# Block sums of three weight matrices: DRAM transfers, or adds in SBUF beside the split

## The chip, the cores and the metric

One core of a Trainium2 chip runs the whole program in one launch. The metric is the device time of one execution in microseconds (us), lower is better. A change of under 0.3% (7.1 us) counts here as no change.

## What is computed

A decoder layer on 1024 tokens of width 1024, in float32. Cut to its matrix products (`u` is the normalised and modulated input):

```python
mod = silu(c) @ w_ada + b_ada                       # 6 rows: shift, scale, gate, twice
hq, hf, hi, hg, rq, rk, rv, rg, ga, gb = split(u @ w_in)
ya = hgrn2(hq, hf, hi, hg) @ w_pa                   # 8 recurrent heads, chunks of 64
yb = retention(rq, rk, rv, rg) @ w_pb               # 4 heads, chunks of 128, gated by silu(rg)
x  = layer_norm(a * x + (1 + gate1) * ((sigmoid(ga) * ya + sigmoid(gb) * yb) @ w_o))
u  = x * (1 + scale2) + shift2
x  = layer_norm(a * x + (1 + gate2) * (square(relu(u @ w_up + b_up)) @ w_down + b_down))
```

## The kernel before

Every float32 operand is split into a high and a low half (`split`, L180-182: ACT copies the high half, DVE subtracts it to get the low one), and every product is three matmuls, high by high, high by low, low by high (`mm3`, L184-194, whose matmuls stand in the profile at L186, L187 and L188).

**Stages, by time in the profiled execution.** To 67 us the start; to about 650 us the HGRN2 heads, with the projection of `ga` at their end; to 1175 us the four retention heads (`r_head`); to 1427 us the gates (`gates`: `gb` in two parts of 256 columns, `rg` in four); then the merge with `w_pa` and `w_pb`, `w_o` (from 1635 us), the up projection (1748 to 2060 us, eight parts) and the down projection.

**Seven products.** Gates, merge, up and down projection use a scheme of seven block products instead of eight. It needs, of a weight with blocks w11, w12, w21, w22, four sums beside three plain blocks: `q5` = w21+w22, `q6` = w11+w21+w22, `q7` = w11+w21, `q3` = w12 + `q6`'s sum; `q1`, `q2`, `q4` are w11, w12, w22. The activations have the like sums, made by DVE (`t_sums`, L932 to L948) as the stage begins. A part of the gates or of the up projection is worked on in the order q1 q5 q6 q2 q7 q3 q4; the first two parts together begin q1 q1 q2 q2, then q5 q6 q7 q3 q4 of the one and of the other (the lead parts below). Each product is 24 matmuls of 128x512.

**Who makes the sums of the weights.** `block_sums` (L197-218) writes, for all six weights (28 parts), four copies and four accumulating transfers of 512 KB from DRAM to DRAM, issued on POOL's queue (L207, L208): 224 transfers. `mm3` paces them: after every `PREP` = 14 x 512 columns of matmuls the next transfer is issued, and it waits for the matmul of that moment (`after`, L226). They begin at 70.5 us and the last is issued at 1166 us, in the order `gb`, `rg`, `pa`, `pb`, `up`, `dn`. In the dense stretches one goes out about every 3.4 us. DMA work of the stages that POOL issues (takes and puts of head outputs, small rows) stands in the same queue.

**The weight stream.** Weights come in pieces of 512 KB through SP's queue into tiles `raw` with three buffers (`_load`, L271-276), always up to three pieces ahead; `_split_to` (L278) splits each piece into `wh` and `wl`, three buffers each, two tiles ahead of the product that asks for one (`W`, L301). In the retention stage the stream also holds the pieces of `w_ada` for the second half of the layer: DVE multiplies them straight out of `raw` (`ada_step`, L378; `ada_group`, L897), eight steps to a group, in order with the rest of its work. The names in the profile's rows: `in_w_ada`, `in_w_in`, `in_w_up` are weights in DRAM, `up_s`, `dn_s`, `gb_s`, `rg_s` their sums, `psa` to `psd` PSUM banks, `ru` the activation sums, `q5h`/`q5l` and so on their halves, `o` a product's copy in SBUF, `hv` the head outputs that the gates take back from DRAM.

Of the kernel before, what the change touches and what calls it, by code (L numbers as in the profile page):

```python
# [9 lines left out]
F32 = mybir.dt.float32  # L10
# [4 lines left out]
ALU = mybir.AluOpType  # L15
# [3 lines left out]
P = 128  # L19
# [12 lines left out]
C_RQ, C_RK, C_RV, C_RG = 4096, 5120, 6144, 8192  # L32
C_GA, C_GB = 10240, 11264
# [28 lines left out]
DN_ORDER = ("q1", "q5", "q6", "q3", "q7", "q2", "q4")  # L62
SECOND = ("q2", "q5", "q3")


def group_steps(parts):

# [5 lines left out]
GATE_STEPS = group_steps([("gb", p) for p in range(2)] + [("rg", p) for p in range(4)])  # L73
UP_STEPS = group_steps([("up", p) for p in range(8)])
LAST = 4
PREP = 14 * 512

H_DEFER = (3, 8)
H_ORDER = (("hq", "hf", "hg", "hi"), ("hg", "hi", "hq", "hf"))
# [68 lines left out]
class Trunk:  # L148
# [45 lines left out]
        return r, l  # L194


    def block_sums(self, name, w, cut, n):  # L197


        nc = self.nc  # L200
        kh, nh = w.shape[0] // 2, w.shape[1] // 2
        st = (nh if cut else kh) // n
        part = (lambda a, p: a[:, st * p:st * (p + 1)]) if cut else (lambda a, p: a[st * p:st * (p + 1), :])
        w11, w12, w21, w22 = ([part(w[k * kh:(k + 1) * kh, m * nh:(m + 1) * nh], p) for p in range(n)]
                              for m in (0, 1) for k in (0, 1))
        s1, s2, s3, s4 = ([self.dp.tile(list(w11[0].shape), F32, name=f"{name}_s{j}_{p}") for p in range(n)] for j in range(1, 5))
        copy = lambda d, a: self.sums.append((0, lambda: nc.gpsimd.dma_start(d, a)))  # L207
        add = lambda late, d, a: self.sums.append((late, lambda: nc.gpsimd.dma_start(d, a, accum_op=ALU.add, max_dma_last_dim=8192)))  # L208
        for p in range(n):
            copy(s1[p], w21[p])  # L210
            copy(s2[p], w11[p])
            copy(s3[p], w11[p])
            copy(s4[p], w12[p])
            add(1, s1[p], w22[p])
            add(1, s3[p], w21[p])
# [28 lines left out]
    def spec_N(self, w, r0, c0, key):  # L244
# [2 lines left out]
        tiles = [(key + (i,), [((lambda d: d.rearrange("p (k c) -> p k c", k=4)), i, (lambda a: a))]) for i in (0, 1)]  # L247
        return pcs, tiles

    def spec_1(self, ap, key):  # L250
        return [ap], [(key, [((lambda d, a=ap: d if len(a.shape) == 2 else d.rearrange("p (k c) -> p k c", k=a.shape[1])), 0, (lambda a: a))])]

    def build_stream(self, specs):
        self.w_tiles = []
        self.w_pcs = []
        for pcs, tiles in specs:
            base = len(self.w_pcs)
            self.w_pcs += pcs
            for key, ops in tiles:
                self.w_tiles.append((key, [(d, base + i, s) for d, i, s in ops]))  # L260
        self.w_raw = {}
        self.w_dst = {}
        self.w_done = {}
        self.w_next = self.w_split = self.w_load = 0
# [13 lines left out]
    def _split_to(self, n):  # L278
        while self.w_split < min(n, len(self.w_tiles)):
            key, ops = self.w_tiles[self.w_split]  # L280
            self._load_to(max(i for _, i, _ in ops) + 3)
            if key[0] == "ada":
                self.w_done[self.w_split] = [self.w_raw[i] for _, i, _ in ops]
                self.w_split += 1
                continue
            if key[0] == "wo":
                self.split(self.woh[key[1]], self.wol[key[1]], self.w_raw[ops[0][1]])
                self.w_done[self.w_split] = None
                self.w_split += 1
# [1148 lines left out]
def build(ctx, tc, ins, out):  # L1438
    k = Trunk(ctx, tc, ins, out)
# [25 lines left out]
    specs = []  # L1465
# [13 lines left out]
                pcs = [ins["w_ada"][512 * i:512 * i + 512, c0:c0 + 256].rearrange("(k p) c -> p k c", p=P) for i in (0, 1)]  # L1479
                specs.append((pcs, [(("ada", s, g), [(None, 0, None), (None, 1, None)])]))  # L1480
    k.sums = []
    wv = {}
    for name, w, cut, n in (("gb", w_in[:, C_GB:C_GB + 1024], 1, 2), ("rg", w_in[:, C_RG:C_RG + 2048], 1, 4),
                            ("pa", ins["w_pa"], 0, 2), ("pb", ins["w_pb"], 0, 4),
                            ("up", ins["w_up"], 1, 8), ("dn", ins["w_down"], 0, 8)):
        wv[name] = k.block_sums(name, w, cut, n)
    parts = lambda q, name, p: k.spec_1(wv[name][q][p].rearrange("(k p) c -> p k c", p=P), (q, name, p))
    specs += [parts(*x) for x in GATE_STEPS]
# [5 lines left out]
    specs += [parts(*x) for x in UP_STEPS]  # L1494
# [89 lines left out]
```

## Time and profile before

| | |
|---|---|
| median of 3 runs | 2366.55 us (2365.38 to 2372.89) |
| the profiled execution | 2367.19 us, its span 2365.4 us |
| TensorE (PE) busy | 2302.0 us, 97% of the span |
| VectorE (DVE) / ScalarE (ACT) / GpSimd (POOL) busy | 1496.8 / 911.4 / 362.8 us |
| moved by DMA | 460.94 MB, 195 GB/s over the span |

PE, DVE, ACT and POOL are the engines; POOLq and SPq are the queues that GpSimd and SyncE issue DMAs from, PEld is PE's weight load. In a row of a timeline stand the start, the duration, the engine and the line, the operation, what it writes and reads, and in brackets how long the engine stood idle before it and what released it. A row with x2 stands for two instructions in a run. A window's row has, for its stretch, each engine's busy time with the number of instructions, the granted TensorE clock as a share of full speed, the share of time that the 16 DMA engines were busy, and GB/s.

### The profile page before, as it was taken

Reading aid. Unit: us, or ns where it says so; the run is one execution under the profiler, and the core shown is the slowest. Engines: PE = TensorE matmul, PEld = TensorE weight load, DVE = VectorE, ACT = ScalarE, POOL = GpSimd, SP = SyncE. Lnnn points to the kernel's source line nnn. Section 1 sums busy time; section 2 is a strip of 40 time slices with the busy share of each in tenths; the row PEclk is TensorE's granted clock in tenths of the full one; section 3 lists DMA queues with packets and bytes.
Section 4 is the critical chain, followed back from the end, with each engine's and each line's share of the span. In section 5 each row is a group of like instructions: output and inputs, shape, how many; then the busy total and the mean of one; then the engine's idle time right before and its main releaser. Section 6 shows DMA issues by size and latency. Waiting matters only on the chain.

```text
span 2365.4 us, 31820 instructions
## 1 busy us (share of the span) xinstructions
PE 2302.0 (97%) x12146; PEld 1970.3 (83%) x12146; DVE 1496.8 (63%) x2684; ACT 911.4 (39%) x1425; POOL 362.8 (15%) x543
## 2 busy tenths in 40 slices
PE   7999999999999999999989999999999999999998
PEld 5888888988779898998978887888888888888886
DVE  7886756577274746556485676667786444544578
ACT  4522222221223232433454444453456555544332
POOL 0222221222312222221232211000000000000000
PEclk9999999999999999999999999999999999999999
DMA  9757565656884967758667867776226464865674
GB/s 268 188 148 163 145 149 152 150 135 161 229 225 107 226 174 175 209 140 228 137 207 246 289 231 277 267 262 231 85 99 218 165 222 161 311 219 190 210 239 155
DMA packets 260361, 460.94 MB, mean 195 GB/s; under 512 B 15488, under 2 KB 158064, under 8 KB 253552
## 3 DMA queue, kind: packets, MB, share of 16 engines
q0 software_dynamic: 65600, 213.42, 33.9%
q1 hardware_dynamic: 194288, 245.04, 31.7%
q8 instruction: 95, 1.56, 0.3%
q14 instruction: 58, 0.48, 0.1%
q10 hardware_dynamic: 320, 0.45, 0.1%
HBM read 380.20 MB, written 196.09 MB: 244 GB/s over the span
## 4 chain that ended last, share of the span: by engine, by line
PE 87%; DVE 7%; DMA 4%; issue 1%; POOL 1%; ACT 1%; ACTq 0%; DVEq 0%; SPq 0%; POOLq 0%
PE psd L188 17%; PE psd L187 17%; PE psd L186 17%; PE psc L186 4%; PE psc L188 4%; PE psc L187 4%; PE psa L188 3%; PE psa L187 3%; PE psa L186 3%; PE psa L590 3%; PE psb L866 3%; DMA raw<-in_w_ada 3%; PE psc L853 2%; PE psb L186 1%; PE psb L187 1%; PE psb L188 1%
## 5 line engine op out<-in xcount | busy, mean ns | idle before, releaser
L182 DVE TENSOR_TENSOR wl<-raw,wh 128x1024 fp32r<-128x1024 f32 (+1 forms) x312 | 328.1, 1057 | 276.4 <-ACT wh L181 272.1
L181 ACT ACTIVATE wh<-raw 128x1024 fp32r<-128x1024 f32 (+1 forms) x312 | 287.8, 929 | 442.0 <-PE psd L187 239.8
L186 PE MATMUL psd<-uh,wh 128*128 128x512 f32 x788 | 315.9, 402 | 0.0
L187 PE MATMUL psd<-ul,wh 128*128 128x512 f32 x788 | 314.2, 399 | 0.4 <-DVE ul L182 0.4
L188 PE MATMUL psd<-uh,wl 128*128 128x512 f32 x788 | 314.2, 399 | 0.0
L186 PE MATMUL psd<-wh,uh 128*128 128x256 f32 x768 | 221.0, 288 | 0.0
L187 PE MATMUL psd<-wl,uh 128*128 128x256 f32 x768 | 218.3, 284 | 0.0
L188 PE MATMUL psd<-wh,ul 128*128 128x256 f32 x768 | 218.1, 284 | 0.0
L182 DVE TENSOR_TENSOR hl<-hr,hh 128x1024 fp32r<-128x1024 f32 x96 | 117.1, 1221 | 132.8 <-ACT hh L181 132.8
L187 PEld LDWEIGHTS psd<-ul,wh 128*128 128x128 f32 x788 | 149.5, 190 | 28.8 <-DVE ul L182 1.2
L188 PEld LDWEIGHTS psd<-uh,wl 128*128 128x128 f32 x788 | 149.4, 190 | 28.5
L186 PEld LDWEIGHTS psd<-uh,wh 128*128 128x128 f32 x788 | 149.1, 190 | 28.3 <-ACT uh L181 0.7
L181 ACT ACTIVATE hh<-hr 128x1024 fp32r<-128x1024 f32 x96 | 101.4, 1056 | 178.9 <-PE psb L187 68.1
L186 PEld LDWEIGHTS psd<-wh,uh 128*128 128x128 f32 x768 | 147.0, 191 | 2.9 <-issue 2.6
L187 PEld LDWEIGHTS psd<-wl,uh 128*128 128x128 f32 x768 | 147.0, 191 | 0.4
L188 PEld LDWEIGHTS psd<-wh,ul 128*128 128x128 f32 x768 | 147.1, 191 | 0.0
L597 DVE COPY_PREDICATED hS<-mask,psa 128x128 f32<-128x128 uint8 x288 | 77.2, 314 | 28.5 <-PE psa L590 25.9
L823 DVE SCALAR_TENSOR_TENSOR vl<-psd,cst,vh 128x256 fp32r<-128x256 f32 x64 | 30.8, 482 | 76.0 <-ACT vh L822 76.0
L822 ACT ACTIVATE vh<-psd,cst 128x256 fp32r<-128x256 f32 x64 | 30.3, 474 | 117.0 <-PE psd L188 114.6
L590 PE MATMUL psa<-qp,k 128*128 128x192 f32 x384 | 72.6, 329 | 1.3 <-DVE k L566 1.3
L590 PEld LDWEIGHTS psa<-qp,k 128*128 128x128 f32 x384 | 62.1, 189 | 10.4 <-issue 5.0
L1253 POOL TENSOR_TENSOR rs<-rs,mhalf 128x1 f32<-128x1 f32 x16 | 12.0, 747 | 369.9 <-DVE rs L1252 340.5
(503 smaller groups left out, 5687.2 us busy)
## 6 DMA issues: line engine op xcount, KB each, us to landing
raw<-in_w_in SPq DMA_DIRECT2D x90, 512.0 KB, 5.2
hr<-hv_d SPq DMA_DIRECT2D x56, 512.0 KB, 3.5
up_s<-in_w_up POOLq DMA_DIRECT2D x48, 512.0 KB, 5.8
dn_s<-in_w_down POOLq DMA_DIRECT2D x48, 512.0 KB, 5.4
hv_d<-hv POOLq DMA_DIRECT2D x16, 1280.0 KB, 5.8
raw<-in_w_ada SPq DMA_DIRECT2D x32, 512.0 KB, 6.5
raw<-up_s SPq DMA_DIRECT2D x32, 512.0 KB, 6.0
raw<-dn_s SPq DMA_DIRECT2D x32, 512.0 KB, 4.4
```

The lines of the kernel that those rows point to most:

```text
L181: self.nc.scalar.activation(hi, src, AF.Copy)
L182: self.nc.vector.tensor_tensor(lo, src, hi.bitcast(F32), op=ALU.subtract)
L186: r = mm(out, wh, uh, start=start, stop=False, skip_group_check=more)
L187: mm(out, wh, ul, start=False, stop=False, skip_group_check=more)
L188: l = mm(out, wl, uh, start=False, stop=stop, skip_group_check=more)
L590: nc.tensor.matmul(pa[:, c * 192:(c + 1) * 192].rearrange("p (b w r) -> p b w r", w=2, r=3 * sz), k[:, n * P:(n + 1) * P], mv, start=True, ...
L597: V.copy_predicated(dst, self.mask8[:, o:o + 128].rearrange("p (b two s) -> p b two s", two=2, s=sz), src)
L822: nc.scalar.activation(hi, pd, AF.Copy, scale=sc)
L823: nc.vector.scalar_tensor_tensor(lo, pd, sc, hi.bitcast(F32), op0=ALU.mult, op1=ALU.subtract)
L853: mm(G[e], l[:, n % 2, es], r, start=n == 0 and i == 0, stop=i == 2, skip_group_check=n > 0)
L866: mm(po, l, r, start=i == 0, stop=i == len(pairs) - 1)
L1253: nc.gpsimd.tensor_tensor(rs, rs, self.mhalf[:, :1], op=ALU.pow)
```

## The change

The sums of `gb`, `rg` and `up` leave `block_sums`; 14 of the 28 parts stay there (`pa`, `pb`, `dn`), 112 transfers instead of 224, and `PREP` is doubled, so that the last is issued where it was. The sums of the three weights are made in SBUF as the stream splits them (`spec_sums`, `sum_split`): for `q5` two blocks are loaded and DVE adds them into two half tiles `ws`, for `q6` w11 is loaded and added to `ws`, for `q7` two blocks are loaded and added in place, and for `q3` nothing is loaded: `q2`'s piece is added to `ws` when it is split, or, in the lead parts, where q2 has gone before q6, w12 is loaded a second time. Each part has four more adds of 128x1024 in all on DVE (those on `ws` as two of 128x512), the splits of q5, q6 and q3 go in halves, and a part has one load more, a lead part two. SP issues 18 loads more, DVE 140 rows more.

```diff
-PREP = 14 * 512
+PREP = 28 * 512
...
+    def spec_sums(self, w, steps):
+        kh, nh = w.shape[0] // 2, w.shape[1] // 2
+        specs, seen = [], set()
+        for q, name, p in steps:
+            late = q == "q3" and (name, p, "q2", "early") in seen
+            if q == "q2" and (name, p, "q6") not in seen:
+                seen.add((name, p, "q2", "early"))
+            seen.add((name, p, q))
+            need = [(0, 1)] if late else BLOCKS_OF[q]
...
+    def sum_split(self, q, hi, lo, raws, late):
+        V = self.nc.vector
+        hi, lo = (x.rearrange("p (k c) -> p k c", k=4) for x in (hi, lo))
+        if q in ("q5", "q6", "q3"):
+            if q == "q5":
+                self.ws = [self.gp.tile([P, 2, 256], F32, tag="gate", bufs=2, name=self.uid("ws")) for _ in (0, 1)]
+            for k, s in zip((slice(0, 2), slice(2, 4)), self.ws):
+                if q == "q5":
+                    V.tensor_tensor(s, raws[0][:, k], raws[1][:, k], op=ALU.add)
+                elif q == "q6" or late:
+                    V.tensor_tensor(s, s, raws[0][:, k], op=ALU.add)
+                self.split(hi[:, k], lo[:, k], s)
+            return
+        if q == "q7":
+            V.tensor_tensor(raws[0], raws[0], raws[1], op=ALU.add)
+        self.split(hi, lo, raws[0])
+        if q == "q2" and self.ws_open:
+            for k, s in zip((slice(0, 2), slice(2, 4)), self.ws):
+                V.tensor_tensor(s, s, raws[0][:, k], op=ALU.add)
...
-    for name, w, cut, n in (("gb", w_in[:, C_GB:C_GB + 1024], 1, 2), ("rg", w_in[:, C_RG:C_RG + 2048], 1, 4),
-                            ("pa", ins["w_pa"], 0, 2), ("pb", ins["w_pb"], 0, 4),
-                            ("up", ins["w_up"], 1, 8), ("dn", ins["w_down"], 0, 8)):
-        wv[name] = k.block_sums(name, w, cut, n)
+    for name, w, n in (("pa", ins["w_pa"], 2), ("pb", ins["w_pb"], 4), ("dn", ins["w_down"], 8)):
+        wv[name] = k.block_sums(name, w, n)
```

Elsewhere the order of DVE differs in the HGRN2 stage from 130 to 200 us, where rows that make the rotary tables (`rot`, L704 to L728) stand later among the rows of the heads, and where each part of `rg` and `up` has its adds. Line numbers shift by up to 46 in the changed kernel (L182 becomes L185, L994 L1040, L956 L1002).

**DVE where the gates begin, about 1200 us.** Before, from the weight split of q5 of gb's first part to the low half of q7's activations:

```order
L182 TENSOR_TENSOR wl_11852<-raw_11673,wh_11851 128x1024
L182 TENSOR_TENSOR q6l_11792<-ru_11774,q6h_11791 128x1024 x2
L994 TENSOR_TENSOR o_11801<-o_11801,psa_11855 128x512
L994 TENSOR_TENSOR o_11803<-o_11803,psa_11871 128x512
L941 TENSOR_TENSOR ru_11775<-ru_11774,ru_11775 128x1024 x2
L182 TENSOR_TENSOR wl_11896<-raw_11805,wh_11895 128x1024
L182 TENSOR_TENSOR q7l_11788<-ru_11775,q7h_11787 128x1024 x2
```

In the changed kernel, from the first add of q5's two blocks to the second add for q6's second half:

```order
L276 TENSOR_TENSOR ws_11687<-raw_11505,raw_11637 128x512
L185 TENSOR_TENSOR q6l_11624<-ru_11606,q6h_11623 128x1024 x2
L185 TENSOR_TENSOR wl_11686<-ws_11687,wh_11685 128x512
L276 TENSOR_TENSOR ws_11688<-raw_11505,raw_11637 128x512
L1040 TENSOR_TENSOR o_11633<-o_11633,psa_11695 128x512
L1040 TENSOR_TENSOR o_11635<-o_11635,psa_11711 128x512
L185 TENSOR_TENSOR wl_11686<-ws_11688,wh_11685 128x512
L987 TENSOR_TENSOR ru_11607<-ru_11606,ru_11607 128x1024 x2
L278 TENSOR_TENSOR ws_11687<-ws_11687,raw_11681 128x512
L185 TENSOR_TENSOR q7l_11620<-ru_11607,q7h_11619 128x1024 x2
L185 TENSOR_TENSOR wl_11736<-ws_11687,wh_11735 128x512
L278 TENSOR_TENSOR ws_11688<-ws_11688,raw_11681 128x512
```

The low half of q6's weights (wl_11896, now wl_11736) stood ahead of the two `q7l` rows, and its first half now stands behind them. On PE, in both kernels, four matmuls of q6 that need only the high half stand first, then one that needs this low half, and q5's 24 matmuls begin two to five rows behind it.

**DVE some 20 us later.** Before, from the weights of q3 and q4 of the first part to the take of the head outputs:

```order
L182 TENSOR_TENSOR wl_11978<-raw_11893,wh_11977 128x1024
L182 TENSOR_TENSOR wl_12012<-raw_11935,wh_12011 128x1024
L956 TENSOR_TENSOR hv_12081<-hv_12081 128x512
L958 TENSOR_TENSOR hv_12081<-hv_12081 128x512
L998 TENSOR_TENSOR o_11954<-o_11954,psd_11679 128x512
```

In the changed kernel, from q7's split on:

```order
L185 TENSOR_TENSOR wl_11784<-raw_11683,wh_11783 128x1024
L278 TENSOR_TENSOR ws_11687<-ws_11687,raw_11779 128x512
L278 TENSOR_TENSOR ws_11688<-ws_11688,raw_11779 128x512
L1002 TENSOR_TENSOR hv_11940<-hv_11940 128x512
L185 TENSOR_TENSOR wl_11825<-ws_11687,wh_11824 128x512
L185 TENSOR_TENSOR wl_11863<-raw_11781,wh_11862 128x1024
L185 TENSOR_TENSOR wl_11825<-ws_11688,wh_11824 128x512
```

The weights of q3 (wl_11978, now the two halves of wl_11825) and q4 (wl_12012, now wl_11863) stood ahead of the first row that reads `hv`; now they stand behind it, and q3's second half stands behind q4's.

More of the change, by code (lines that the diff above doesn't have):

```diff
@@ L63 @@
 SECOND = ("q2", "q5", "q3")
+BLOCKS_OF = {"q1": [(0, 0)], "q2": [(0, 1)], "q3": [], "q4": [(1, 1)], "q5": [(1, 0), (1, 1)], "q6": [(0, 0)], "q7": [(0, 0), (1, 0)]}
+GROUPS = ("gb", "rg", "up")
 def group_steps(parts):
@@ L194, in mm3, with block_sums @@
         return r, l
-    def block_sums(self, name, w, cut, n):
+    def block_sums(self, name, w, n):
         nc = self.nc
         kh, nh = w.shape[0] // 2, w.shape[1] // 2
-        st = (nh if cut else kh) // n
-        part = (lambda a, p: a[:, st * p:st * (p + 1)]) if cut else (lambda a, p: a[st * p:st * (p + 1), :])
+        st = kh // n
+        part = lambda a, p: a[st * p:st * (p + 1), :]
         w11, w12, w21, w22 = ([part(w[k * kh:(k + 1) * kh, m * nh:(m + 1) * nh], p) for p in range(n)]
@@ L248, in spec_N @@
         return pcs, tiles
+    def spec_sums(self, w, steps):
[7 more added lines that the diff above has]
+            need = [(0, 1)] if late else BLOCKS_OF[q]
+            pcs = [w[kh * k:kh * k + kh, nh * m + 256 * p:nh * m + 256 * p + 256].rearrange("(k p) c -> p k c", p=P) for m, k in need]
+            specs.append((pcs, [((q, name, p), [(None, i, late) for i in range(len(pcs))])]))
+        return specs
+    def sum_split(self, q, hi, lo, raws, late):
[17 more added lines that the diff above has]
+                V.tensor_tensor(s, s, raws[0][:, k], op=ALU.add)
     def spec_1(self, ap, key):
@@ L260, in build_stream @@
                 self.w_tiles.append((key, [(d, base + i, s) for d, i, s in ops]))
+        self.ws_open = False
         self.w_raw = {}
@@ L280, in _split_to @@
             key, ops = self.w_tiles[self.w_split]
-            self._load_to(max(i for _, i, _ in ops) + 3)
+            if ops:
+                self._load_to(max(i for _, i, _ in ops) + 3)
             if key[0] == "ada":
@@ L295, in _split_to @@
                 lo = self.wp.tile([P, 1024], F32R, tag="wl", bufs=3, name=self.uid("wl"))
+            if key[1] in GROUPS:
+                q = key[0]
+                late = q == "q3" and bool(ops)
+                self.ws_open = q == "q6" or self.ws_open and q != "q3"
+                self.sum_split(q, hi, lo, [self.w_raw[i] for _, i, _ in ops], late)
+                ops = []
             for d, i, s in ops:
@@ L1481, in build @@
     k.sums = []
-    wv = {}
-    for name, w, cut, n in (("gb", w_in[:, C_GB:C_GB + 1024], 1, 2), ("rg", w_in[:, C_RG:C_RG + 2048], 1, 4),
-                            ("pa", ins["w_pa"], 0, 2), ("pb", ins["w_pb"], 0, 4),
-                            ("up", ins["w_up"], 1, 8), ("dn", ins["w_down"], 0, 8)):
-        wv[name] = k.block_sums(name, w, cut, n)
+    wv, gate = {}, {}
+    for name, w, n in (("pa", ins["w_pa"], 2), ("pb", ins["w_pb"], 4), ("dn", ins["w_down"], 8)):
+        wv[name] = k.block_sums(name, w, n)
     parts = lambda q, name, p: k.spec_1(wv[name][q][p].rearrange("(k p) c -> p k c", p=P), (q, name, p))
-    specs += [parts(*x) for x in GATE_STEPS]
+    for name, c0, n in (("gb", C_GB, 1024), ("rg", C_RG, 2048)):
+        gate[name] = iter(k.spec_sums(w_in[:, c0:c0 + n], [x for x in GATE_STEPS if x[1] == name]))
+    specs += [next(gate[x[1]]) for x in GATE_STEPS]
     specs += [parts(q, "pa", p) for q in MERGE_ORDER for p in range(2)]
@@ L1493, in build @@
             specs.append(k.spec_1(ins["w_o"][n // 3 * P:(n // 3 + 1) * P, :], ("wo", n // 3)))
-    specs += [parts(*x) for x in UP_STEPS]
+    specs += k.spec_sums(ins["w_up"], UP_STEPS)
     specs += [parts(q, "dn", p) for q in DN_ORDER for p in range(8)]
```

## Prediction

> **What bounds the kernel now.** The profile's first part and the chain of work that ended last say the same: the matmuls do.
>
> ```profile
> PE 2302.0 (97%) x12146; PEld 1970.3 (83%) x12146; DVE 1496.8 (63%) x2684; ACT 911.4 (39%) x1425; POOL 362.8 (15%) x543
> ...
> PE 87%; DVE 7%; DMA 4%; issue 1%; POOL 1%; ACT 1%; ACTq 0%; DVEq 0%; SPq 0%; POOLq 0%
> ```
>
> PE works 2302.0 of 2365.4 us and the change takes no matmul away, so it can win or lose only in the remaining 63 us and in the clock. The waits of PE, sorted by time, begin with these:
>
> ```profile
> PE psa L776 <- DVE t L762: 9.0, 3, 5.0
> PE psa L554 <- DVE hS L558: 5.8, 5, 2.9
> PE psd L188 <- DVE wl L182: 5.4, 2, 5.0
> ```
>
> The first and the third lie in two stages that the change touches: L776 is in the retention heads, `psd` L188 is the start of the gates. PE's timeline shows the single stalls:
>
> ```profile
> 135.52 0.89 PE L554 MATMUL psa<-q,k 128*128 128x192 f32 x4 [2.88 <-DVE hS L558]
> ...
> 707.07 0.58 PE L853 MATMUL psc<-vh,knh 128*128 128x256 f32 x1 [4.29 <-DVE gl L182]
> ...
> 943.97 0.69 PE L776 MATMUL psa<-cst,t 128*128 128x128 f32 x2 [5.04 <-DVE t L762]
> ...
> 1078.07 0.41 PE L776 MATMUL psa<-cst,t 128*128 128x128 f32 x2 [2.89 <-DVE t L762]
> ```
>
> In the retention stage that is 4.29 + 5.04 + 2.89 = 12.2 us. What DVE itself stood at just before each of them is in DVE's timeline and in the chain:
>
> ```profile
> 702.25 2.05 DVE L378 SCALAR_TENSOR_TENSOR acc<-raw,cond,acc 128x256 f32<-128x256 f32 x4 [4.56 <-DMA raw<-in_w_ada]
> ...
> 940.07 2.05 DVE L378 SCALAR_TENSOR_TENSOR acc<-raw,cond,acc 128x256 f32<-128x256 f32 x4 [6.52 <-DMA raw<-in_w_ada]
> ...
> 929.47 10.50 DMA raw<-in_w_ada
> ```
>
> DVE works in order and stands at `ada_step` for a piece of `w_ada`; the rows that PE needs are queued behind it. The piece took 10.50 us from issue to landing at 929.47. The list of DMA issues, with the KB of one and the median us to landing, shows what such a piece takes elsewhere:
>
> ```profile
> raw<-in_w_ada SPq DMA_DIRECT2D x32, 512.0 KB, 6.5
> ...
> raw<-in_w_up SPq DMA_DIRECT2D x24, 512.0 KB, 3.8
> ```
>
> `in_w_up` is read by the stream in the up projection, from about 1740 us, long after the last sum was issued; its 3.8 us is this kernel's price for a piece with no sums beside it. In the retention stage the sums of `up` and `dn` run beside the loads, and the windows show it:
>
> ```profile
> core 0: us, PE busy (x) PEld busy (x) DVE busy (x) ACT busy (x) POOL busy (x), PEclk, DMA share, GB/s
> 675.00:700.00 25.00, 24.23 (x167) 21.71 (x166) 19.35 (x34) 7.57 (x12) 4.93 (x6) 1.00 0.97 238
> 700.00:725.00 25.00, 20.71 (x159) 19.94 (x158) 12.21 (x30) 8.16 (x21) 1.89 (x3) 0.93 0.48 159
> 925.00:950.00 25.00, 19.96 (x88) 16.48 (x86) 16.93 (x31) 4.72 (x7) 3.68 (x5) 0.86 0.80 184
> 1075.00:1100.00 25.00, 21.64 (x133) 19.14 (x133) 19.55 (x34) 7.70 (x12) 3.07 (x4) 0.93 0.71 201
> 1200.00:1225.00 25.00, 18.50 (x73) 14.11 (x72) 22.50 (x23) 13.01 (x17) 6.42 (x12) 0.86 0.50 169
> 1425.00:1450.00 25.00, 23.03 (x95) 18.57 (x94) 18.48 (x22) 9.72 (x11) 4.17 (x8) 0.93 0.89 314
> 1307.50:1345.00 37.50, 37.50 (x167) 31.07 (x166) 26.48 (x38) 15.19 (x21) 6.41 (x12) 1.00 0.71 245
> 1867.50:1905.00 37.50, 37.50 (x168) 31.03 (x167) 17.61 (x21) 20.43 (x30) 2.12 (x4) 1.00 0.54 189
> ```
>
> The DMA engines are 97% busy just before the stall at 703 and 80% around the one at 939. The column before that share is the granted clock. It dips where PE stood still, and that costs extra: in 1425:1450 PE did 95 matmuls of 128x512, where the undisturbed 1307.5:1345 has 167 in 37.5 us, 0.225 us each. 95 of them are 21.3 us, the window's idle time is 25 - 23.03 = 1.97 us, and the missing 1.7 us went to the slower clock.
>
> **The retention stage, gain.** The transfers fall from 224 to 112 over the same time, so half as many meet a load. I take the piece halfway between 10.5 us and the undisturbed 3.8, about 7.2, so 3.3 us earlier, and the rows behind it with it. That takes 3.3 of the 4.29, 3.3 of the 5.04, all of the 2.89: 9.5 us. What remains of the stalls, 1.0 and 1.7 us, is under the 1.97 that still cost clock, so the three dips go as well, 3 x 1.7 = 5.1. Sum 14.6, taken as 15. The upper end is 12.2 + 5.1 = 17.3, if nothing waits any longer. The lower end is 4: a landing that gains only half of 6.5 - 3.8, 1.3 us, in each of the three, and no dip undone.
>
> The row of the clock stands against a rule. In the Trainium skill, "TensorE: Matmul & The Clock Gate", Part 1, the array goes to half clock after an idle window of about 3.4 us; by that the 2.89 us stall would have cost no clock, and the gain would be some 1.7 us smaller. The window from 1425, with a dip after 1.97 us, does not agree, and I go by the row.
>
> **The HGRN2 stage, gain.** At 132.6 us PE waits 2.88 us for `hS`, on a DVE that at that time is working through the rotary tables; in the new order their rows stand later. Between nothing (another row of the same head is late next) and 2.88 + 1.7 = 4.6. I take 3. POOL's queue carries half the sums there too, which I count with it.
>
> **The start of the gates, cost.** Here DVE is the chain, as its rows and PE's show:
>
> ```profile
> 1200.20 1.22 DVE L182 TENSOR_TENSOR wl<-raw,wh 128x1024 fp32r<-128x1024 f32 x1
> 1201.33 2.35 DVE L182 TENSOR_TENSOR q6l<-ru,q6h 128x1024 fp32r<-128x1024 f32 x2
> 1203.61 1.28 DVE L994 TENSOR_TENSOR o<-o,psa 128x512 f32<-128x512 f32 x2
> 1204.80 2.35 DVE L941 TENSOR_TENSOR ru<-ru,ru 128x1024 f32<-128x1024 f32 x2
> 1207.07 1.22 DVE L182 TENSOR_TENSOR wl<-raw,wh 128x1024 fp32r<-128x1024 f32 x1
> ...
> 1208.34 0.80 PE L188 MATMUL psd<-q6h,wl 128*128 128x512 f32 x1 [5.00 <-DVE wl L182]
> ```
>
> From one start to the next a row of 128x1024 takes 1.14 us, one of 128x512 0.60. PE stands for 5.00 us until q6's low half is there, at 1208.3. In the new order there come, from 1200.2 on: the first add on `ws` 0.6, two `q6l` 2.3, half a split 0.6, the second add 0.6, two outputs 1.2, half a split 0.6, L941's two rows 2.3, an add 0.6, two `q7l` 2.3, half a split 0.6. That is 11.7 and ends at 1211.9, so PE goes on 3.5 us later. Nothing covers this: DVE has no gap between those rows. With a little clock I take 4.
>
> Some 20 us on, DVE's new order has q3's two halves behind the first row on `hv`, and the second of them behind q4's split. Before, that row stood here:
>
> ```profile
> 1224.56 0.69 DVE L956 TENSOR_TENSOR hv<-hv 128x512 f32<-128x512 f32 x1 [2.05 <-DMA hv<-oh_d]
> ```
>
> PE reaches q7 of the first part at about 1223.5 in my replay of the rows, q3 24 matmuls (5.4 us) later, at 1229, and q3's second half by 1231.7. q4's piece can be loaded only when q7's split has freed a buffer, at about 1223.3; it lands between 3.8 and 10.5 us later, needs 2.1 for both halves of its split, and q3's second half 0.6: 1229.8 to 1236.5, so 0 to 4.8 us late. I take 2, nearer the short landings. The second lead part has the same figure again behind the next take, with the same prices and one more `hv` landing in it: 0 to 8, taken as 2.5. Together the gates cost 4 + 2 + 2.5 = 8.5, between 3.5 and 16.5.
>
> **Steady parts, no cost.** A part is 37.5 us on PE. DVE is busy 26.48 of them with `rg` (1307.5) and 17.61 with `up` (1867.5). The four adds are 4 x 1.14 = 4.6 us, halves of splits a few tenths, so 31.4 and 22.5: still covered. If `rg`'s cover failed, each of four parts could lose a load's lateness, 1 or 2 us. The one load more per part is 1 in 8 of the stream at a DMA share of 0.71 and hidden. At the start of the up projection I see nothing that comes out clearly either way: between -1.5 and +1.5, taken at 0.
>
> **Sum.** -15 - 3 + 8.5 = -9.5 us. The profiled execution took 2367.19 us, 1.8 more than its span and 0.64 more than the median of 2366.55. From the median it gives 2357.0 us. The ends of this case are -17.3 - 4.6 + 3.5 = -18.4 (2348) and about -4 (2362), with costs and gains a little worse than taken.
>
> **Rivals.**
>
> *The loads stay late: no change.* Half as many sums need not shorten a wait by half. A load that meets a sum is slowed as before, and the stalls are two or three single loads out of 32. If those meet a sum again, or if SP's own pieces ahead of them make up the 10.5 us, the stage gives 4 to 7 us and no dip is undone. With -5.5 - 2 + 8.5 = +1 this gives 2367.5. For it: the median of 32 landings is 6.5, so much of the time sums do no harm, and the bad ones come singly. Against it: a DMA share of 0.97 ahead of the first. The Trainium skill, "DMA: Bandwidth & Descriptors", Queues, rings and completion order, says that each DMA engine takes turns between the queues' rows packet by packet; by that a load beside a running sum is slowed as much at half the density, which is this rival; no row of this trace tells it from the forecast.
>
> *The gates lose more: slower.* DVE now stands at rows that wait for head outputs and for second blocks, with the splits of the next products queued behind. If both lead parts pay the upper figures (16.5) and the retention stage gives its lower one (4) and the HGRN2 stage nothing, the sum is +12.5: 2379. It ends above the bound for slower as soon as the gates' cost exceeds the gains by 7.1 us. For it: pieces in the gates' first 75 us share the engines with takes and puts of head outputs; against it, the upper figures need a landing of 10 us at two places at once.
>
> *It doesn't do what it says*, so that the three sums' cost merely moves to the steady parts of `rg`: four parts at 2 us, +8 on top of the forecast, 2365. I count it with the first.
>
> **How the numbers follow.** The forecast 0.58, the loads stay late 0.27, the gates lose more 0.15. The bounds of no change are 2359.5 and 2373.7. Of the forecast's 2348 to 2362 some 0.11 lies above 2359.5, so faster is 0.47 plus 0.03 from the first rival's better end, 0.50; slower is 0.13, since a few of the third's cases stay below 2373.7; no change is the remaining 0.37. The range goes from 2346 to 2372: it takes in the forecast and the first rival and leaves out most of the slower one. The forecast alone has 2348 to 2362.
>
> **What would show it.** Right: no stall over 2 us on PE between 650 and 1175 us, a clock of 1.00 in the windows that hold 703, 939 and 1076, a median landing of `w_ada` pieces near 5; at the gates' first stall an idle time near 8 in place of 5.00, and small stalls for q3 or q4 within the next 50 us; 31 us of DVE in a 37.5 us window of `rg`, with PE full. Wrong: DVE still standing over 4 us at L378's row in the new kernel, which is the first rival; or stalls of 4 us and more behind rows on `hv`, which is the second; or PE idle in the steady parts.

## The result, and the profile after

Over 20 runs each the changed kernel took 2374.48 us (2366.81 to 2377.77), the kernel before 2366.84 us (2361.02 to 2377.43). The ratio is 1.0027, 95% interval 1.0016 to 1.0037: about 6 us slower (the medians lie 7.6 us apart), which is just under the 0.3% that counts as a change, but on the other side from the forecast and above its range of 2346 to 2372. One execution of a later kernel, `second_own` below, had a granted clock of 0.655 and took 3269.55 us, and that kernel's ratio is of its other ten runs. The profiled execution took 2375.38 us, its span 2373.4.

The changed kernel's page, its engines and its chain:

```profile
PE 2304.5 (97%) x12146; PEld 1971.2 (83%) x12146; DVE 1564.7 (66%) x2824; ACT 915.1 (39%) x1469; POOL 275.0 (12%) x431
...
PE 79%; DVE 10%; DMA 6%; issue 2%; ACT 1%; POOL 1%; ACTq 0%; DVEq 0%; SPq 0%; POOLq 0%
```

PE does the same work; DVE has 68 us more of it, and its share and DMA's in the chain have grown. The stalls of PE in the retention stage are gone but for one of 1.18 us, and others stand in their place. PE's timeline of the changed kernel has these, from 650 us to the up projection: the one left in the retention stage and all over 3 us (the idle time is in the bracket):

```profile
696.67 0.39 PE L899 MATMUL psc<-vh,knh 128*128 128x256 f32 x1 [1.18 <-DVE gl L185]
...
1184.15 0.77 PE L189 MATMUL psd<-q6h,wh 128*128 128x512 f32 x1 [9.50 <-issue]
...
1240.26 0.50 PE L189 MATMUL psd<-q4h,wh 128*128 128x512 f32 x1 [3.71 <-DVE o L1044]
...
1264.73 0.79 PE L191 MATMUL psd<-q6h,wl 128*128 128x512 f32 x1 [4.45 <-DVE wl L185]
...
1423.52 0.80 PE L190 MATMUL psd<-hl,wh 128*128 128x512 f32 x1 [4.18 <-DVE hl L185]
...
1647.24 0.77 PE L189 MATMUL psd<-woh,yh 128*128 128x512 f32 x1 [3.74 <-DVE y L1191]
...
1811.59 0.80 PE L189 MATMUL psb<-q7h,wh 128*128 128x512 f32 x1 [3.07 <-ACT o L1038]
```

The windows of the changed kernel show them with their clock:

```profile
675.00:700.00 25.00, 23.82 (x174) 22.33 (x173) 20.80 (x40) 8.77 (x17) 2.55 (x3) 1.00 0.77 185
925.00:950.00 25.00, 25.00 (x174) 22.43 (x173) 19.85 (x37) 9.97 (x18) 2.46 (x4) 1.00 0.56 166
1175.00:1200.00 25.00, 15.61 (x56) 12.01 (x57) 23.60 (x27) 13.24 (x20) 6.45 (x12) 0.80 0.52 176
1200.00:1225.00 25.00, 25.00 (x112) 20.73 (x111) 17.22 (x26) 10.81 (x18) 4.86 (x9) 1.00 0.88 301
1225.00:1250.00 25.00, 21.29 (x87) 17.12 (x87) 14.42 (x22) 6.43 (x10) 10.33 (x20) 0.93 0.86 292
1250.00:1275.00 25.00, 20.55 (x84) 16.57 (x83) 10.03 (x13) 8.56 (x14) 4.10 (x8) 0.93 0.74 260
1400.00:1425.00 25.00, 19.77 (x83) 15.52 (x82) 25.00 (x35) 12.41 (x17) 2.15 (x4) 0.93 0.68 238
1800.00:1825.00 25.00, 21.93 (x85) 17.65 (x84) 12.72 (x18) 12.21 (x19) 0.65 (x2) 0.86 0.72 240
1270.00:1307.50 37.50, 37.50 (x167) 30.95 (x166) 30.97 (x46) 14.45 (x23) 6.41 (x12) 1.00 0.61 210
```

The last row is a part of `rg` as the prediction's sign has it: 31 us of DVE in 37.5, and PE full.

Both traces hold 12146 matmuls in nearly the same order, so the two can be laid over each other: for the n-th matmul, its start in one less its start in the other. How this difference grows over a stage is what the stage lost (plus) or gained (minus). The table has it against the first profile of before, for a second profile of before and for three of the changed kernel (the other two were taken later, as experiments below); stages are cut at the times of before.

| us | before, again | after | after, again | after, third | forecast |
|---|---|---|---|---|---|
| start, to 120 | -0.6 | -1.9 | -0.5 | -2.4 | 0 |
| HGRN2 heads, to 650 | +0.7 | -4.2 | -2.5 | -2.4 | -3 |
| retention, to 1199 | +0.2 | -19.9 | -17.6 | -20.3 | -15 |
| gates' first stall, to 1230 | +0.6 | +4.1 | +3.6 | +4.4 | +4 |
| gb's two parts, to 1262 | 0.0 | +5.6 | +7.3 | +5.9 | +4.5 |
| rg's first part, to 1300 | 0.0 | +6.3 | +6.1 | +3.2 | 0 |
| rg's middle, to 1395 | 0.0 | +0.6 | +0.6 | +0.1 | 0 |
| rg's end and merge's start, to 1450 | +0.2 | +4.4 | +4.9 | +4.6 | 0 |
| the gates in all | +0.8 | +20.9 | +22.5 | +18.2 | +8.5 |
| `w_o`, 1625 to 1748 | +0.1 | +4.0 | +3.0 | +4.1 | 0 |
| up projection, to 2050 | -0.4 | +5.8 | +4.8 | +3.6 | 0 |
| down projection and tail | +1.1 | +3.3 | +2.5 | +2.8 | 0 |

So the retention stage gave more than was forecast, the gates took all of it back, and the up projection and two places behind the merge (`w_o` and the tail) made the loss. Each column is one execution.

### The profile page after: what moved, and what is told of

Same layout as the page of the kernel before. It is cut to its first block, busy times and chain, and to the rows that moved or that the text cites. A ratio compares the mean times of both kernels' runs of the same rounds, so it can differ in the third digit from the quotient of the medians.

```text
span 2373.4 us, 31839 instructions
## 1 busy us (share of the span) xinstructions
PE 2304.5 (97%) x12146; PEld 1971.2 (83%) x12146; DVE 1564.7 (66%) x2824; ACT 915.1 (39%) x1469; POOL 275.0 (12%) x431
## 3 DMA queue, kind: packets, MB, share of 16 engines
q0 software_dynamic: 40512, 154.70, 22.5%
## 4 chain that ended last, share of the span: by engine, by line
PE 79%; DVE 10%; DMA 6%; issue 2%; ACT 1%; POOL 1%; ACTq 0%; DVEq 0%; SPq 0%; POOLq 0%
PE psd L189 16%; PE psd L190 16%; PE psd L191 16%; PE psc L189 3%; PE psc L190 3%; PE psc L191 3%; PE psa L636 3%; PE psb L912 3%; PE psa L191 2%; PE psa L190 2%; PE psa L189 2%; DMA raw<-in_w_in 2%; DVE wl L185 2%; PE psc L899 2%; PE psb L189 1%
## 5 line engine op out<-in xcount | busy, mean ns | idle before, releaser
L185 DVE TENSOR_TENSOR wl<-raw,wh 128x1024 fp32r<-128x1024 f32 (+1 forms) x270 | 276.8, 1031 | 177.0 <-ACT wh L184 171.3
L184 ACT ACTIVATE wh<-raw 128x1024 fp32r<-128x1024 f32 (+1 forms) x270 | 243.2, 908 | 389.0 <-PE psd L190 196.9
L185 DVE TENSOR_TENSOR hl<-hr,hh 128x1024 fp32r<-128x1024 f32 x96 | 117.2, 1222 | 135.3 <-ACT hh L184 135.3
L185 DVE TENSOR_TENSOR wl<-ws,wh 128x512 fp32r<-128x512 f32 x84 | 56.0, 688 | 31.5 <-ACT wh L184 31.2
```

The lines of the kernel that those rows point to most:

```text
L184: self.nc.scalar.activation(hi, src, AF.Copy)
L185: self.nc.vector.tensor_tensor(lo, src, hi.bitcast(F32), op=ALU.subtract)
```

## The experiments

**Which stage's sums cost: up alone, the gates alone.** `up_only` makes gb's and rg's sums in DRAM again:

```diff
-GROUPS = ("gb", "rg", "up")
-PREP = 28 * 512
+GROUPS = ("up",)
+PREP = 19 * 512
...
-    for name, w, n in (("pa", ...), ("pb", ...), ("dn", ...)):
+    for name, w, cut, n in (("gb", ...), ("rg", ...), ("pa", ...), ("pb", ...), ("dn", ...)):
...
```

> The sums of gb and rg are made in DRAM again, only up's in SBUF: 160 transfers, one after every 19 x 512 columns. Theory A (the retention stage gains by fewer transfers beside its loads; the gates lose by their own weights, two pieces to a sum through three buffers with DVE in order): the retention stage keeps some 12 of its 20 us, the gates take what they took before (within 3 us), the up projection loses 4 to 6; 2355 to 2362 us, about 9 under the kernel before. Rival B (the gates give back whatever comes in early, since they wait for something with its own clock, such as the head outputs' takes or the DMA share after a shorter retention stage): the gates lose 10 us or more here too, and the time is 2366 or more.

Measured 2359.47 us, ratio to before 0.9968 (0.9955 to 0.9980). By stage: HGRN2 +0.2, retention -14.8, gates +0.3, `w_o` +2.8, up +6.3. The gates' stalls are again those of before, while the retention stage handed over 17 us early:

```profile
1191.56 0.80 PE L191 MATMUL psd<-q6h,wl 128*128 128x512 f32 x1 [5.00 <-DVE wl L185]
...
1799.42 0.79 PE L189 MATMUL psb<-q7h,wh 128*128 128x512 f32 x1 [3.15 <-ACT o L1038]
```

Rival B falls: what comes in early is kept, when the gates' sums are not in SBUF. `gates_only` is the mirror (`GROUPS = ("gb", "rg")`, up's sums in `block_sums`, `PREP = 17 * 512`).

> The mirror: gb's and rg's sums in SBUF, up's in DRAM, 176 transfers, one after every 17 x 512 columns. Theory A: the retention stage gains 5 to 10 us, the gates lose 15 to 21, the up projection is as before; 2374 to 2380. Rival B: as much is lost at the gates as was gained ahead of them, 5 to 10, and the time is 2366 to 2370.

Measured 2385.62 us, ratio 1.0091 (1.0071 to 1.0112), beyond what either theory said. Retention -12.2, gates +22.9, `w_o` +0.5, up 0.0. The gates lost nearly twice what the retention stage gained, with the same stalls at the same rows as the changed kernel:

```profile
1199.83 0.77 PE L189 MATMUL psd<-q6h,wh 128*128 128x512 f32 x1 [9.42 <-issue]
...
1255.09 0.78 PE L189 MATMUL psd<-q4h,wh 128*128 128x512 f32 x1 [3.49 <-DVE o L1044]
...
1281.57 0.80 PE L191 MATMUL psd<-q6h,wl 128*128 128x512 f32 x1 [6.45 <-DVE wl L185]
...
1441.25 0.79 PE L190 MATMUL psd<-hl,wh 128*128 128x512 f32 x1 [4.19 <-DVE hl L185]
```

The rest of its excess stands in the HGRN2 stage (+4.4, one stall of 7.05 us at the place where before has 2.88; DVE stands just ahead of it for 4.27 us until a put of the rotary tables to DRAM has landed). So the gates' 21 us belong to gb's and rg's sums in SBUF, the up projection's 5 to up's.

**The retention stage: transfers beside the loads, or another order.** `prep14` is the changed kernel with `PREP = 14 * 512`.

> The changed kernel with the old spacing of 14 x 512: the 112 transfers are out by about 620 us and none runs in the retention stage. If the transfers beside the loads made the retention stage's stalls, it has none over 1 us here as well and gains 19 to 22 us; the HGRN2 stage gives back up to 4 us of its 4.2. 2371 to 2379, within 4 of the changed kernel. If the gain came from the new order of rows instead, spacing changes nothing in either stage.

Measured 2375.33 us, ratio 1.0039 (1.0025 to 1.0053). Retention -18.7, HGRN2 -0.7, gates +21.9, up +6.0. What a piece of `w_ada` took from issue to landing is in the lists of DMA issues of gates_only, up_only, the changed kernel and prep14, in this order (before has 6.5):

```profile
raw<-in_w_ada SPq DMA_DIRECT2D x32, 512.0 KB, 5.2
```

```profile
raw<-in_w_ada SPq DMA_DIRECT2D x32, 512.0 KB, 4.9
```

```profile
raw<-in_w_ada SPq DMA_DIRECT2D x32, 512.0 KB, 4.1
```

```profile
raw<-in_w_ada SPq DMA_DIRECT2D x32, 512.0 KB, 3.9
```

And DVE's waits for them (us in all, times, the longest), before and in the changed kernel:

```profile
DVE acc L378 <- DMA raw<-in_w_ada: 19.6, 7, 6.5
```

```profile
DVE acc L424 <- DMA raw<-in_w_ada: 1.4, 1, 1.4
```

With 224, 176, 160 and 112 transfers over the same stretch a piece lands in 6.5, 5.2, 4.9 and 4.1 us, and with none beside it in 3.9; the longest single wait falls from 6.5 us to 1.4. The stage gains 12.2, 14.8 and 19.9. The kernels further down fall in between: 7.2 with 176 transfers, 15.0 with 160, 14.7 with 152, 13.5 with 144, 17.9 with 128. Having no transfers there at all (prep14) gains no more than having half of them, 18.7, and one stall of 1.37 us is left where none over 1 us was expected. prep14 alone doesn't tell the transfers from a new order of rows, since it has the changed kernel's order there. But that order is the old one: between 650 and 1170 us DVE works through the same rows in the same order before and after the change, but for two rows moved by a few places at 1036 us. With the order the same and the gain growing as the transfers get fewer, that the sums made these stalls is shown. In the HGRN2 stage the closer spacing leaves 0.7 us of a gain of 2.4 to 4.2, as expected; DVE's order of rows differs there between the two kernels, so that the spacing is the cause isn't shown.

**Are the late pieces the gates' cost?** `one_block` leaves the second pieces out, and w12's second load with them, so its sums are of other blocks than the layer's:

```diff
-BLOCKS_OF = {..., "q5": [(1, 0), (1, 1)], "q6": [(0, 0)], "q7": [(0, 0), (1, 0)]}
+BLOCKS_OF = {..., "q5": [(1, 0)], "q6": [(0, 0)], "q7": [(0, 0)]}
...
-                    V.tensor_tensor(s, raws[0][:, k], raws[1][:, k], op=ALU.add)
+                    V.tensor_tensor(s, raws[0][:, k], raws[0][:, k], op=ALU.add)
...
```

> The changed kernel with the second pieces of q5 and q7 and the second load of w12 left out (the first piece is added to itself, so every row of DVE and ACT stays): part of the weights is not read. Theory A: the stalls behind late pieces go, the gates lose 4 to 9 us instead of 21, the up projection 1 instead of 6; 2354 to 2362. Rival C (DVE's adds, the halves and their places behind the rows on hv cost, whatever the loads do): the gates still lose 15 or more; 2370 or more.

Measured 2364.41 us, ratio to before 0.9986 (0.9970 to 1.0002), between the two theories. Its gates lose 19.1 us in all, which is what rival C expected of them, but not where the changed kernel loses: gb's two parts 0.0 and rg's first part 0.0, where the changed kernel lost 5.6 and 6.3, and up -2.7 where it lost 5.8; but the gates' first stall 4.5 and rg's end 3.0 stay, and rg's middle lost 11.6, which neither theory had. Those stalls are of another kind. DVE's timeline in one_block, as the second part of rg begins:

```profile
1305.53 0.69 DVE L276 TENSOR_TENSOR ws<-raw 128x512 f32<-128x512 f32 x1 [5.32 <-DMA raw<-in_w_in]
...
1307.47 0.68 DVE L1040 TENSOR_TENSOR o<-o,psa 128x512 f32<-128x512 f32 x1
```

The first add of the next part's q5 now stands ahead of the outputs of the part before (L1040 and what follows), and DVE waits 5.32 us there for a piece; in the changed kernel that add stands behind most of those outputs. The order of DVE's rows is fixed in a kernel (all three profiles of the changed kernel have the same one), and with fewer loads it came out otherwise, so this kernel isn't the changed one less its late pieces. What it shows is that without second pieces three stalls are gone: at gb's q4, at rg's first q6 and in the up projection's lead parts.

**One buffer more.** `second_own` gives the second pieces of q5 and q7 a buffer of their own; to make room, the outputs `o` have one buffer less in the gates:

```diff
+        if i in self.w_second and self.x_pool is not None:
+            t = self.x_pool.tile([P, 1024], F32, tag="raw2", bufs=1, name=self.uid("rawx"))
...
-                self.fo, self.o_bufs = self.pool("fo", "right", fo), 9
+                self.fo, self.o_bufs = self.pool("fo", "right", fo), 8
+                self.x_pool = self.fo
...
```

> The changed kernel with one buffer more, for the second pieces of q5 and q7 alone (in the pool of the outputs, where o has 8 buffers instead of 9 to make room). If the three buffers make the pieces late, the gates lose 6 to 12 us instead of 21 and up's lead 0 to 4 instead of 6: 2356 to 2366. If the pieces are late since the DMA engines are shared in that stretch, or DVE's order behind the takes decides, nothing changes by over 3 us: 2370 to 2377.

Measured 2368.82 us, ratio 1.0019 (1.0002 to 1.0036), between the two again. Its profile is of another execution of the same kernel, 2368.71 us.

> second_own once more for its profile. Its median was 5.7 us under the changed kernel's. If the buffer made the pieces late, what is won lies at rg's first part (6.3 us lost in the changed kernel, here 0 to 3) and at up's lead (5.6, here 0 to 3), and the waits of DVE for pieces of in_w_in in the gates are under half of the changed kernel's; if not, it lies anywhere, in the HGRN2 stage for one.

By stage: gb's two parts +1.8, rg's first part 0.0, up +0.1, as the buffer theory has it; but rg's middle +17.3, at the first matmul of a part:

```profile
1289.90 0.79 PE L189 MATMUL psd<-uh,wh 128*128 128x512 f32 x1 [4.17 <-DVE o L1071]
...
1333.81 0.80 PE L189 MATMUL psd<-uh,wh 128*128 128x512 f32 x1 [4.20 <-DVE o L1071]
...
1377.29 0.50 PE L189 MATMUL psd<-uh,wh 128*128 128x512 f32 x1 [3.57 <-DVE o L1071]
```

They look like one_block's stalls: DVE's waits for pieces of `in_w_in` at the q5 add come to 20.7 us in five places (17.8 in one_block, 3.9 in the changed kernel), ahead of the rows that free PSUM; and one_block has them with nine buffers for `o`, so the buffer taken from `o` isn't needed for them. DVE's waits for all pieces in the gates are 22.9 us against the changed kernel's 25.9, where under half was expected: that expectation fell, and the gates lose 20.5 us in all. So the pieces' buffers do matter at rg's first part and up's lead, and easing them alone brings a new wait of the same worth.

**Which parts.** The next five leave single parts in SBUF (a list of name and part decides in `sum_split`, `spec_sums` and `block_sums`):

```diff
+IN_SBUF = [("rg", p) for p in (0, 1, 2, 3)] + [("up", p) for p in range(8)]       # mix_rg_up, PREP 24
+IN_SBUF = [("rg", p) for p in (1, 2, 3)] + [("up", p) for p in range(2, 8)]       # mix_late, PREP 20
+IN_SBUF = [("up", p) for p in range(2, 8)]                                        # mix_up6, PREP 17
+IN_SBUF = [("rg", p) for p in (1, 2)] + [("up", p) for p in range(2, 8)]          # mix_rg12_up6, PREP 19
+IN_SBUF = [("rg", p) for p in (1, 2)] + [("up", p) for p in range(8)]             # mix_rg12_up, PREP 21
-            if key[1] in GROUPS:
+            if key[1:] in IN_SBUF:
```

> Only gb's two parts go back to sums in DRAM; rg and up stay in SBUF: 128 transfers, one after every 24 x 512 columns. Theory A': the start of the gates (4 us) and the stall of the second lead part (5.6) belong to gb's own sums and go, and so does the 6.3 us stall at rg's first part if it is the knock-on of DVE standing behind the take; rg's end and the up projection's lead stay as in the changed kernel. Gates 0 to 6 instead of 21, the whole 2353 to 2362. Rival: each part with sums in SBUF costs where it stands, rg's first part by its own two-piece loads; then the gates still lose 9 to 12 and the whole is 2363 or more.

> Only the steady parts in SBUF: rg's parts 2 to 4 and up's parts 3 to 8; gb, rg's first and up's two lead parts in DRAM: 152 transfers, one after every 20 x 512. Theory A': no lead part loads two pieces, so gates and up lose under 5 us together, and the retention stage keeps about 15 of 20: 2350 to 2357, the best so far. If the steady parts cost by DVE's adds, their cost is at rg's end: 3 us more there, and the whole is 2357 to 2361.

> Only up's six steady parts in SBUF, 176 transfers, one after every 17 x 512: the retention stage gains 10 to 13, gates and up nothing lost; 2353 to 2360. Against up_only it wins up's lead (6 us) and loses some of the retention stage (3 us).

> Only steady parts that neither begin nor end a stage are in SBUF: rg's second and third, up's third to eighth. 160 transfers, one after every 19 x 512 columns, as in up_only. If lead parts and rg's last part are what costs, gates, merge start and up lose under 2 us together; HGRN2 and retention stage gain what up_only's gained (17 us together): 2351 to 2357, below up_only's 2359.5. If any part in SBUF costs its share (1.5 us for each of the gates' parts at DVE's adds), 2357 or more.

> The same with up's two lead parts in SBUF too: 144 transfers, one after every 21 x 512. Up's lead loses 5 to 6 us as in up_only and in the changed kernel, the rest as in mix_rg12_up6: 2355 to 2361.

| us | mix_rg_up | mix_late | mix_up6 | mix_rg12_up6 | mix_rg12_up |
|---|---|---|---|---|---|
| median | 2369.66 | 2361.62 | 2365.75 | 2357.71 | 2366.92 |
| ratio to before | 1.0012 | 0.9982 | 0.9993 | 0.9952 | 0.9999 |
| interval | 0.9996 to 1.0029 | 0.9968 to 0.9997 | 0.9976 to 1.0011 | 0.9935 to 0.9970 | 0.9982 to 1.0015 |
| HGRN2 | +1.5 | +1.4 | +4.4 | +0.6 | +1.4 |
| retention | -17.9 | -14.7 | -7.2 | -15.0 | -13.5 |
| first stall and gb | +1.6 | +0.7 | +0.5 | 0.0 | 0.0 |
| rg's first part | +4.1 | 0.0 | 0.0 | 0.0 | 0.0 |
| rg's end, merge's start | +3.7 | +4.1 | +0.7 | +2.1 | +0.6 |
| `w_o` | +5.7 | +3.7 | +3.3 | +3.1 | +3.3 |
| up | +4.7 | -1.0 | -0.5 | +0.1 | +4.8 |
| down and tail | +1.6 | +0.4 | +2.8 | +2.3 | +7.3 |

(`start, to 120` and rg's middle, -2.9 to +0.2 and 0.0 to +0.8, are left out.) Each cost goes with its part. gb in DRAM: the growth of the first stall and gb's stall go (1.6 of 9.7 us left). rg's first part in SBUF: 4.1 us, so most of it is its own and not the knock-on of gb's, as the rival had it; the expectation of mix_rg_up fell there. rg's last part in SBUF: 3.7 to 5.3 us at the end of rg (the 4.2 us stall at `hl`, in mix_rg_up and mix_late as in the changed kernel); without it 0.6 to 2.1. Up's two lead parts in SBUF: 3.6 to 6.3 in all kernels that have them there with three buffers; without them none. Steady parts of either weight cost nothing that shows. mix_rg12_up6 beats both kernels, 2357.71 us, 0.7 above its expected range; up_only's 2359.47 can't be told from it. mix_late came out 5 us above what was expected, with rg's end and `w_o` still lost. mix_rg_up did 8 above, where its rival had it, mix_up6 and mix_rg12_up 6, these two not where the change of parts lies: mix_up6 in the HGRN2 stage (a stall of 7.90 us at 138 us, behind 4.35 us in which DVE waits for a put of the rotary tables) and the retention stage, mix_rg12_up behind the up projection. mix_up6's runs lie in two groups, four from 2354.46 to 2359.66 and eight from 2364.52 to 2371.27; its profile is of one in the upper group, and what the lower ones do is not known.

**What comes back.** Two more profiles of the changed kernel and one more of before, with no edit:

> The kernel before once more, for what a second profile of the same order of rows shows. Stalls that the order sets should come back within 1 us (4.3 at 703, 5.0 at 939, 5.0 at 1203, 2.0 at 1427); the one at 1648 us, behind loads of single rows, was 1.05 before and between 1.05 and 4.3 in the kernels since, and should move by over 1 us here too if it is chance.

> The changed kernel once more, for a second profile of the same order of rows. If the stalls in the gates are set by order and buffers, they come back: 9.5 us at the gates' first q6, 3 to 5 at the second lead part's q4, 3 to 6 at rg's first part, 21 us lost in the stage within 3. Behind the merge the first profile lost 4.1 us more at 1648 (single rows' loads), 1.1 at 2059 and 1.8 in the tail; what of that is the change's comes back, what is chance moves by over 1 us.

> A third profile of the changed kernel, with the same expectation: the gates' 21 us and up's lead of 5.6 within 3 and 1.5 us, the three places behind the merge anywhere between 0 and what the first profile showed if they are chance, close to it (within 1 us) if not.

Their columns are in the first table (2369.22, 2379.40 and 2370.69 us). The stalls of before came back at 4.34, 6.93, 5.01 and 2.19 us (703, 939, 1203, 1427), so that at 939 moved by 1.9 us where under 1 was expected, and that at 1648 at 1.18, so it is not chance in this kernel. The changed kernel's stalls in the gates came back at 9.50 and 9.49, 4.33 and 3.99, 4.21 and 2.86 us; the last, and up's 3.6 us in the third profile, are a little below what was expected. It lost at `w_o` 4.0, 3.0 and 4.1 us (stalls of 3.74, 2.46 and 3.61) and in the tail, behind the last matmul, 1.8 each time: these come back with it, though it changes no row there.

## Why the prediction was wrong

**The retention stage: right in its mechanism, too small.** Half the transfers took the stalls away. It gained 17.6 to 20.3 us where 15 was taken and 17.3 called the upper end. The windows of the stage from its first to its last matmul, before and after, with PE's busy time, clock and DMA share:

```profile
650.00:1199.00 549.00, 534.23 (x3651) 491.25 (x3650) 326.02 (x663) 185.75 (x382) 126.19 (x177) 0.99 0.70 179
```

```profile
643.90:1173.00 529.10, 527.51 (x3651) 486.93 (x3650) 326.23 (x663) 183.78 (x380) 83.46 (x122) 1.00 0.49 133
```

PE's idle time fell from 14.8 to 1.6 us, 13.2 where the sum had 9.5, and the clock gave the other 6.7 or so where it had 5.1. Two terms were mis-sized. The landing: "halfway between 10.5 us and the undisturbed 3.8" left stalls of 1.0 and 1.7 us, but the 32 pieces now land in 4.1 at the median, next to prep14's 3.9, and one stall of 1.18 is left; small stalls that the sum did not list (0.57, 1.03) went too. And the dips: "3 x 1.7" took all three alike, but the window at 925 was at 0.86, twice as far under full speed as the other two at 0.93. The Trainium skill's rule of the queues' turns ("DMA: Bandwidth & Descriptors", Queues, rings and completion order), on which the first rival leant, doesn't decide here: DVE's waits for the pieces fell from 19.6 us to 1.4, far below half.

**The HGRN2 stage: near in the number, by luck in part.** -2.4 to -4.2 for -3. But the stall for `hS`, which the new order was to take away, is still 2.07 to 2.13 us (2.88 and 3.47 before) and gave 0.8. Another 1.5 in the first profile is the dip of the clock there, which the other two still have, and 1.1 lie between 180 and 200 us, where the second profile of before is 0.8 earlier as well. Later kernels of this document, with DVE's order moved there in much the same way, have stalls of 2.2 to 7.9 us at that place.

**The gates' first stall: right.** PE went on 3.6 to 4.4 us later for 4. One detail was wrong: q6's high half, too, now hangs on `ws`, so PE stands once for 9.50 us and not twice.

**gb's two parts: near in the sum, wrong in the place and the path.** Nothing was lost at q3 of the first part (2 taken). At q4 of the second (2.5 taken, of 0 to 8) it was 5.6 to 7.3. DVE's timeline of the changed kernel:

```profile
1235.98 0.69 DVE L1002 TENSOR_TENSOR hv<-hv 128x512 f32<-128x512 f32 x1 [8.67 <-DMA hv<-oh_d]
...
1239.53 0.68 DVE L1044 TENSOR_TENSOR o<-o,psd 128x512 f32<-128x512 f32 x1
...
1253.69 1.29 DVE L278 TENSOR_TENSOR ws<-ws,raw 128x512 f32<-128x512 f32 x2 [3.91 <-DMA raw<-in_w_in]
...
1262.85 1.23 DVE L282 TENSOR_TENSOR raw<-raw,raw 128x1024 f32<-128x1024 f32 x1 [7.00 <-DMA raw<-in_w_in]
```

The row that PE waits for, L1044, stands behind a row that reads `hv` and kept DVE for 8.67 us. That alone is not new. Before, the same row, L998, stood behind a wait of 9.67 us for the same take:

```profile
1248.66 0.69 DVE L956 TENSOR_TENSOR hv<-hv 128x512 f32<-128x512 f32 x1 [9.67 <-DMA hv<-oh_d]
...
1256.14 0.68 DVE L998 TENSOR_TENSOR o<-o,psd 128x512 f32<-128x512 f32 x1
```

PE came to its matmul only at 1258.26, 9.6 us after that take had ended DVE's wait. In the changed kernel PE would have come at 1236.55 and DVE's wait ended at 1235.98, so the take is about 9 us later for PE. Its transfers didn't take longer (7.80 us for the last of the first four, 8.32 before); they were issued later. The rows of DVE and POOL show why:

```profile
1221.14 1.29 DVE L278 TENSOR_TENSOR ws<-ws,raw 128x512 f32<-128x512 f32 x2 [3.25 <-DMA raw<-in_w_in]
...
1225.67 0.54 POOL L1006 DMA_DIRECT2D av_d<-hv  x1 [1.45 <-DVE hv L1003]
...
1226.92 1.60 POOL L1078 DMA_DIRECT2D hv<-oh_d  x3
```

POOL issues the takes in order with the puts of the rows on `hv` (av_d), and these wait for DVE. From the first of the rows on `hv` to the last of the first two groups DVE needs 24.8 us (1200.63 to 1225.40) where it needed 9.5 before (1224.56 to 1234.08): 7.2 of them are waits for pieces of `in_w_in` (2.25, 1.65 and 3.25), the rest are mostly adds and splits that now stand in between. So gb's stall, too, begins in part with late pieces. That it is gone in one_block, and gb's loss down to 1.8 us in second_own, agrees, though both have another order of rows.

**"Steady parts, no cost" is the step that failed, with the zero at the up projection.** The sum compared DVE's 31.4 us with a part's 37.5 and found cover. That holds in the middle parts (0.1 to 0.6 us lost), and fails where a part is not steady. At rg's first part DVE stands 3.91 and 7.00 us for pieces, in the rows above: two of the three buffers go to one sum, and they are freed by DVE, which has just stood for the take. The pieces also take long to land there, as the chain shows, against 3.9 us undisturbed:

```profile
1246.10 7.50 DMA raw<-in_w_in
...
1255.01 7.75 DMA raw<-in_w_in
```

How much of the lateness is the buffers and how much the landing isn't shown. mix_rg_up still has 4.1 us there, with gb's stall behind the take gone, second_own none with one buffer more. At rg's end DVE is busy for all of the 25 us from 1400 and hands `hl` over 4.18 us late; that cost goes with rg's last part. DVE was busy for all of the 25 us ahead of the smaller stall of before, too, so the adds had no cover. In the up projection's lead parts w12's second load and q7's second piece go through the same three buffers, and q4's piece comes late: it is issued when DVE's add for q7 has freed a buffer, and lands 9.20 us later. The chain and ACT's row in the changed kernel:

```profile
1800.71 9.20 DMA raw<-in_w_up
...
1810.00 1.06 ACT L184 ACTIVATE wh<-raw 128x1024 fp32r<-128x1024 f32 x1 [6.28 <-DMA raw<-in_w_up]
```

The prediction had priced exactly this (q4's piece can be loaded only when a split has freed a buffer) for gb's lead parts, where it cost nothing, and not for up's, where it cost 3.6 to 5.8.

**The miss in one sum.** In the first profile the change is +8.0 us where -9.5 was forecast, 17.5 off. rg's parts, taken at nothing, are 11.3 of it, the up projection 5.8, `w_o` and what follows the up projection, of which the sum has no term, 7.3, and the gates' start with gb 1.2; 8.0 more were gained ahead of the gates (retention stage 4.9, HGRN2 stage 1.2, the start 1.9).

**The rivals.** The first fell: the loads did come early. The second, a larger loss at the gates, is what happened, 18 to 22 us where its upper end was 16.5; but it needed the retention stage to gain little, and the gain was full, so the time stayed under its 2379. Its mechanism, DVE standing for head outputs and for second blocks with other rows behind, is gb's loss and rg's first part's, 9 to 13 us of it; the first stall (3.6 to 4.4) and rg's end (4.4 to 4.9) are rows of DVE that nothing covers.

**What stays open.** `w_o` lost 3 to 4 us in every profile of the changed kernel at a stall behind three loads of single rows in a chain; the tail 1.8. No row there is changed. `w_o`'s loss is there in the variants with up in SBUF (2.6 to 5.7) but for prep14 (0.0), and not in gates_only (0.5). The first link of that chain, the rows of `in_b_ada`, took 8.51 us in the changed kernel's first profile and 6.93 in its second, 6.44 before and 6.45 in prep14; in the first, before and prep14 the loads around it are issued at the same distances; why it lands later is open. So is what moves the order of DVE's rows when loads or buffers change.

## What to carry to other kernels

Here half the transfers beside a load that an in-order engine waits for gave back nearly all of the waits, and having none gave no more; count what the longest landing must lose, not the median. A sum moved from DRAM into the split cost little in steady parts and much in those that begin or end a stage, where the same few buffers and the same in-order engine also serve takes, activation sums and the first weights: so move the steady parts and leave the others (2357.7 against 2366.6 and 2374.5 us). A wait that was harmless, such as the one for a take, becomes a stall when what starts it comes later: follow the chain back to its start before naming the row that waits longest as the cause. And price "busy time against a part's time" only where every part is alike; at the ends of a stage replay the rows.

## What the runs showed of the hardware

Stalls of PE came with a lower clock as well: in the window of 25 us with the 9.50 us stall the granted clock was 0.80, in those with one of 3.1 to 4.5 us 0.86 to 0.93. The length of the stall alone doesn't set it: one of 1.97 us in the kernel before had 0.93, one of 2.07 us in the changed kernel 1.00. Over 25 us, 0.93, 0.86 and 0.80 come to about 1.7, 3.5 and 5 us of full speed lost.

A load of 512 KB took 3.9 us at the median with no transfers beside it, and 6.5 in the retention stage of the kernel before, where one transfer of 512 KB was issued every 4.7 us at the median; at 112 transfers instead of 224 it took 4.1. At the parts that lost time single loads took 7.5 to 9.2 us (the rows at 1246, 1255 and 1800 us).
